# Pools in another order so that matmul operands begin at multiples of 64 bytes, and products over 64 rows filled up to 128 rows with zeros

## The chip, the core and the metric

The kernel runs on one core of a Trainium2 chip. The metric is the device time of one execution in microseconds (us); shorter is better. TensorE (PE) multiplies, ScalarE (ACT), VectorE (DVE) and GpSimd (POOL) do the element-wise work, and SyncE (SP) issues the loads. A product on PE has a stationary operand, which a weight load (PEld) brings into the array, and a moving operand, whose columns stream through it. Both come from the on-chip memory SBUF.

## The reference: what is computed

Two layers of an encoder over 256 tokens of width 2048, all in float32. Each layer is one wide projection, three mixers side by side, an output projection, and a feed-forward block:

```python
def hybrid_layer(x, ...):
    h = rms_norm(x, norm_mix)
    z = jnp.einsum('bsd,de->bse', h, w_in)
    ...
    y_a = mlstm_mixer(ml_q, ml_k, ml_v, ml_o, ml_g, ...)        # 4 heads, d_k 64, d_v 128
    y_b = mla_mixer(mla_cq, mla_ckv, ...)                       # 6 heads, 128 + 64 (rope) per head
    y_c = dilated_mixer(dil_q, dil_k, dil_v, ...)               # 6 heads of 128
    y = jnp.concatenate([y_a, y_b, y_c], axis=-1)
    x = x + jnp.einsum('bse,ed->bsd', y, w_out)
    h = rms_norm(x, norm_ff)
    u = jax.nn.relu(jnp.einsum('bsd,df->bsf', h, w_ff1))        # 2048 -> 8192
    return x + jnp.einsum('bsf,fd->bsd', u * u, w_ff2)
```

## The kernel before

**Precision by splitting.** A float32 operand is kept as two float32r parts, `hi` (ACT rounds) and `lo` (DVE subtracts); a product of two such operands is three matmuls, hi·hi, hi·lo and lo·hi. Each element has 4 bytes in either part.

**Weights.** `Weights` streams all weights in one fixed order in tiles of 128 x 1024. SP loads a tile into one of three `wst` buffers, ACT writes `whi`, DVE writes `wlo` (four buffers each), three tiles ahead of PE.

**Products with weights.** `token_group` serves the input projection (moving `whi` or `wlo`, stationary `xg`), the output projection (stationary `y`) and the second feed-forward product (stationary `u`): for each of 16 row blocks and each of two token halves, two matmuls with `whi` and one with `wlo`, 512 columns each (336 in one of the nine input groups). `w_half` serves the first feed-forward product: weights are stationary, and each row block of `xg` moves once with 512 columns (both parts, against `whi`) and once with 256 (the hi part, against `wlo`). All of these write a tile named `g`.

**Mixers.** Their products stand between those of the next input group. They are generators; a planner (`Stream`) with fixed costs for each engine decides, when the program is written, behind which product each step is put. Room in a pool is counted by `take` and `give`: `t2` has 22 tiles of 2,048 bytes, `half` 7 of 1,024. Two of the mixers' products contract over 64 rows only: in `mla_head` the lo part of the rotated keys (`kr[1]`, tile `krl`, 64 x 256) against `qrT_sb`, twice per head, 12 heads in both layers; in `ml_head` the lo part of q (`ml_ql`, 64 x 256) against `ml_k`, twice per head, 8 heads in both layers. Their neighbours contract over 128 rows (hi and lo one above the other).

**Where tiles lie.** Pools lie in SBUF one behind another in the order in which they are opened, and so do the tiles of a pool. Before, `cp` is first, and in it `vec`, whose row has 952 elements: 3,808 bytes, 59.5 times 64. Nearly every tile behind it therefore begins 32 bytes past a multiple of 64: `xg`, `x`, `whi`, `wlo`, `u`, `y`, all operands of the mixers, and the constants. So do all slices of them that a matmul takes. In the pool `big` a buffer has 4,128 bytes (64.5 times 64, set by `ml_va`), so that every other one begins at a multiple of 64; they hold only float32 sources of transposes and `ml_va`. Counted in 2,048 bytes, `xg`, `whi` and `wlo` begin at the same place (736), the tiles of `t2` (`u`, `y`) at another (1,888).

Of the kernel before, what the change touches and what calls it, by code (L numbers as in the profile page):

```python
# [10 lines left out]
F32 = mybir.dt.float32  # L11
F32R = mybir.dt.float32r
AF = mybir.ActivationFunctionType
# [43 lines left out]
V_BIAS = V_DROPE + 4 * DIL_ROT  # L57
V_ON = V_BIAS + 16
V_ALL = V_ON + ML_H * ML_DV


class Ctx:
# [385 lines left out]

def load_vectors(c, l):

    c.vec = c.cp.tile([P, V_ALL], F32, tag="vec", name="vec", bufs=1)
    c.nc.scalar.dma_start(c.vec[:, :V_GF], c.vecs[l, :, :V_GF])

    def rest():
        c.nc.scalar.dma_start(c.vec[:, V_GF:], c.vecs[l, :, V_GF:])

    return rest

# [74 lines left out]
def k_rope(c, z1):  # L533
    nc = c.nc
    yield from c.s.take(half=1)
    ss = c.small.tile([P, 2], F32, tag="kr_ss", name="kr_ss")
    for tt in range(NT):
        nc.scalar.activation(junk(c, MLA_ROPE), z1[:, tt, :MLA_ROPE], AF.Square, accum_out=ss[:, tt:tt + 1])
    yield
    mean_eps(c, ss, ss, MLA_ROPE)  # L540
    y = yield from rsqrt(c, ss, 2)
    kr = c.half.tile([P, NT, MLA_ROPE], F32, tag="half", name="kr")
    nc.vector.tensor_tensor(out=kr, in0=z1[:, :, :MLA_ROPE],
                            in1=y[:, :2].unsqueeze(2).to_broadcast([P, NT, MLA_ROPE]), op=ALU.mult)
    yield
    apply_rope(c, kr, kr, c.rope[:, 2], c.rope[:, 3], NT, MLA_ROPE)
    yield
    tp = yield from bank(c, "krT")
    for tt in range(NT):
        transpose(c, tp[:MLA_ROPE, tt * P:(tt + 1) * P], kr[:, tt])  # L550

    kh = c.cp.tile([P, S], F32R, tag="krh", name="krh", bufs=1)
    kl = c.cp.tile([MLA_ROPE, S], F32R, tag="krl", name="krl", bufs=1)
    yield
    k = tp[:MLA_ROPE, :S]
    nc.scalar.copy(kh[MLA_ROPE:], k)
    split2(c, kh[:MLA_ROPE], kl, k)
    c.s.give(m=1, half=1)
    c.kr = kh, kl

# [53 lines left out]
def mla_head(c, h):  # L614
    nc = c.nc
    WQ = MLA_NOPE + MLA_ROPE
    NK = MLA_QR // P
    yield from c.s.take(**MLA_ROOM)
    hi, lo = c.w.next()
    if h == MLA_H - 1:  # L620
        c.s.give(t2=4)
    ps = []
    for tt in range(NT):
        b = new_bank(c, "mla_z")
        for kt in range(NK + 1):
            if kt < NK:
                o, cs, first, last = b[:, :WQ], slice(kt * WQ, (kt + 1) * WQ), kt == 0, kt == NK - 1
            else:
                o, cs, first, last = b[:, WQ:WQ + 256], slice(NK * WQ, NK * WQ + 256), True, True
            xh = c.lat[kt][:, tt * P:(tt + 1) * P]  # L630
            xl = c.lat[kt][:, S + tt * P:S + (tt + 1) * P]
            mm(c, o, xh, hi[:, cs], first, False)
            mm(c, o, xh, lo[:, cs], False, False)
            mm(c, o, xl, hi[:, cs], False, last)
        ps.append(b)
    yield

    cols = ((0, MLA_NOPE), (WQ, WQ + MLA_NOPE), (MLA_NOPE, WQ))
    ss = c.small.tile([P, 3, 2], F32, tag="mla_ss", name="mla_ss", bufs=4)
    for tt in range(NT):  # L640
        for i, (a, b) in enumerate(cols):
            nc.scalar.activation(junk(c, b - a), ps[tt][:, a:b], AF.Square, accum_out=ss[:, i, tt:tt + 1])
    vh = c.half.tile([P, NT, MLA_V], F32R, tag="half", name="mla_vh")
    vl = c.half.tile([P, NT, MLA_V], F32R, tag="half", name="mla_vl")
    for tt in range(NT):
        src = ps[tt][:, WQ + MLA_NOPE:WQ + 256]
        nc.vector.tensor_copy(vh[:, tt], src)
        nc.vector.tensor_tensor(out=vl[:, tt], in0=src, in1=vh[:, tt].bitcast(F32), op=ALU.subtract)
    yield
    mean_eps(c, ss[:, 0:2], ss[:, 0:2], MLA_NOPE)  # L650
    mean_eps(c, ss[:, 2], ss[:, 2], MLA_ROPE)
    r = yield from rsqrt(c, ss.rearrange("p a b -> p (a b)"), 6)
    qr = c.tmp.tile([P, NT, MLA_ROPE], F32, tag="qr", name="qr", bufs=3)
    a, b = cols[2]
    for tt in range(NT):
        nc.vector.tensor_scalar(out=qr[:, tt], in0=ps[tt][:, a:b], scalar1=r[:, 4 + tt:5 + tt], scalar2=None,
                                op0=ALU.mult)
    yield
    nk = tile2k(c, "nk", F32).rearrange("p (i t d) -> p i t d", i=2, t=NT)
    for i in range(2):  # L660
        a, b = cols[i]
        for tt in range(NT):
            nc.scalar.activation(nk[:, i, tt], ps[tt][:, a:b], AF.Copy, scale=r[:, 2 * i + tt:2 * i + tt + 1])
    c.s.give(m=2)
    apply_rope(c, qr, qr, c.rope[:, 0], c.rope[:, 1], NT, MLA_ROPE)
    yield
    tp = yield from bank(c, "nkT")
    for i in range(2):
        for tt in range(NT):
            transpose(c, tp[:, i * S + tt * P:i * S + (tt + 1) * P], nk[:, i, tt])  # L670
    yield
    q, k = tile2k(c, "mla_q"), tile2k(c, "mla_k")
    split_gains(c, (q, k), tp, V_NOPE)
    c.s.give(m=1)
    yield
    tq = yield from bank(c, "qrT")
    for tt in range(NT):
        transpose(c, tq[:MLA_ROPE, tt * P:(tt + 1) * P], qr[:, tt])
    yield
    qs = c.half.tile([P, S], F32R, tag="half", name="qrT_sb")  # L680
    split2(c, qs[:MLA_ROPE], qs[MLA_ROPE:], tq[:MLA_ROPE, :S])
    c.s.give(m=1)
    yield
    sc = (yield from bank(c, "mla_s")).rearrange("p (t s) -> p t s", t=NT)
    for tt in range(NT):
        t = slice(tt * P, (tt + 1) * P)
        mm3(c, sc[:, tt], (q[:, t], q[:, S:][:, t]), (k[:, :S], k[:, S:]), True, False)
        mm(c, sc[:, tt], qs[:, t], c.kr[0], False, False)
        mm(c, sc[:, tt], qs[:MLA_ROPE, t], c.kr[1], False, True)
    p = yield from softmax(c, sc, (MLA_NOPE + MLA_ROPE) ** -0.5, None)  # L690
    yield from pv(c, p, [(vh[:, st], vl[:, st]) for st in range(NT)], 4 + h, 3)
    c.s.give(half=3)
# [146 lines left out]
def ml_qk(c, ps, rt):  # L839
# [3 lines left out]
    for tt in range(NT):  # L843
        nc.scalar.activation(z[:, tt], ps[tt], AF.Copy, scale=rt[:, tt:tt + 1])
    yield
    yield from c.s.take(t2=4)
    for pr in range(2):
        tp = yield from bank(c, "ml_qkT")
        for j in range(2):
            for tt in range(NT):  # L850
                transpose(c, tp[:, j * S + tt * P:j * S + (tt + 1) * P],
                          z[:, tt, j * 256 + pr * P:j * 256 + (pr + 1) * P])
        yield

        kk = tile2k(c, "ml_k").rearrange("p (h t) -> p h t", h=2)
        qq = tile2k(c, "ml_q").rearrange("p (h t) -> p h t", h=2)
        ql = c.half.tile([P, S], F32R, tag="ml_ql", name="ml_ql", bufs=2)
        q, k = tp[:, :S], tp[:, S:]
        half = [slice(i * ML_DK, (i + 1) * ML_DK) for i in range(2)]
        for i, r in enumerate(half):  # L860
            nc.scalar.copy(kk[r, i], k[r])
            nc.scalar.copy(qq[r, i], q[r])
            nc.scalar.copy(qq[half[1 - i], i], q[r])
        yield
        for i, r in enumerate(half):
            o = half[1 - i]
            nc.vector.tensor_tensor(out=kk[o, i], in0=k[r], in1=kk[r, i].bitcast(F32), op=ALU.subtract)
            nc.vector.tensor_tensor(out=ql[r], in0=q[r], in1=qq[r, i].bitcast(F32), op=ALU.subtract)
            c.mlqk.append((kk[:, i], qq[:, i], kk[r, i], ql[r]))
        c.s.give(m=1)  # L870


def ml_v(c, ps, rt):
    nc = c.nc
    c.va = c.big.tile([P, NT, ML_H, ML_DV + 1], F32, tag="big", name="ml_va")
    nc.gpsimd.memset(c.va[:, :, :, ML_DV:], 1.0)
    yield
    for tt in range(NT):
# [24 lines left out]

def ml_head(c, h):
    nc = c.nc
    kk, qq, kh, ql = c.mlqk[h]
    yield from c.s.take(t2=2, half=1)
    ws = []
    for d in range(2):
# [13 lines left out]
    st = yield from bank(c, "ml_st")  # L923
    for s in range(NT):
        mm(c, st[:, s * S:(s + 1) * S], kk[:, s * P:(s + 1) * P], qq, True, False)
        mm(c, st[:, s * S:(s + 1) * S], kh[:, s * P:(s + 1) * P], ql, False, True)
    yield
    stv = st.rearrange("p (s t) -> p s t", s=NT)
    sc = ML_DK ** -0.5
# [11 lines left out]
    c.s.give(m=1)  # L941
    c.mlqk[h] = None
    if c.mlqk[h ^ 1] is None:
        c.s.give(t2=2)
    hs = c.half.tile([P, NT, ML_DV], F32, tag="half", name="ml_hs")
    ss = c.small.tile([P, 2], F32, tag="ml_ss", name="ml_ss", bufs=4)
    C1 = ML_DV + 1
# [184 lines left out]
def encoder(ctx, tc, xT, x, const, vecs, w_in, w_in1, w_mla, w_out, w_ff1, w_ff2, out):  # L1132
# [7 lines left out]
        vecs, w_in, w_in1, w_mla, w_out, w_ff1, w_ff2, out)  # L1140
    c.B_ST, c.B_HL = 3, 4
    pool = lambda name, bufs, **k: ctx.enter_context(tc.tile_pool(name=name, bufs=bufs, **k))
    c.cp = pool("cp", 1)
    c.small = pool("small", 2)
    c.tmp = pool("tmp", 2)
    c.xp = pool("xp", 1)
    c.wp = pool("wp", 1)
    c.big = pool("big", 4)
    c.half = pool("half", HALF)
    c.t2 = pool("t2", T2)  # L1150
    c.gps = pool("gps", 4, space=PSUM)
    c.mps = pool("mps", 4, space=PSUM)
    ctx.enter_context(tc.manual_schedule())
# [171 lines left out]
```

## Time and profile before

| | |
|---|---|
| median of 3 runs | 2199.95 us (2199.28 to 2200.12) |
| the profiled execution: its own time | 2200.16 us |
| its span (first to last instruction) | 2197.9 us |
| PE busy | 2164.0 us, 98% of the span |
| DVE busy / ACT busy / POOL busy | 1326.9 / 1077.9 / 110.9 us |
| DMA engines | 56.2% busy with the weights' queue, 177 GB/s on average |

The first 33 us are the start, the mixers of the two layers lie at about 33 to 300 us and 1145 to 1390 us, each followed by the output projection (70 us) and four rounds of the two feed-forward products. A PE duration in the profile overlaps the next instruction's, and its end is modelled; the pace of PE is read from the starts.

### The profile page before, as it was taken

The page shows a single profiled execution, that of the slowest core. Times are in us where ns is not written, and L with a number is a line of the kernel's source. Part 1 is how long each engine was busy: PE and PEld are TensorE (multiplying, and loading weights), DVE is VectorE, ACT ScalarE, POOL GpSimd, SP SyncE. Part 2 cuts the span into 40 slices and gives each one's busy share as a digit, 9 for nine tenths or more (in the row PEclk, how much of TensorE's full clock was granted, in tenths as well). Part 3 has the DMA queues.
Part 4 walks back from the last instruction along what each step waited for, and adds up shares of the span by engine and source line. Part 5 has one row for each costly group of instructions (what it writes and reads, how often), then busy time and mean ns, then how long its engine had stood idle before and what let it go on. Part 6 is the DMA issues. An engine that isn't in the chain of part 4 may idle for free.

```text
span 2197.9 us, 28890 instructions
## 1 busy us (share of the span) xinstructions
PE 2164.0 (98%) x10848; PEld 1805.4 (82%) x10848; DVE 1326.9 (60%) x1963; ACT 1077.9 (49%) x1873; POOL 110.9 (5%) x142
## 2 busy tenths in 40 slices
PE   8999999999999999999999999999999999999999
PEld 6787888888888888888887888888888888888887
DVE  7667755655564565565557687556546645655654
ACT  5666655543443444344456666454434434534442
POOL 6112100000000000000001021000000000000000
PEclk9999999999999999999999999999999999999999
DMA  7543455565666656566554434556566666666564
GB/s 233 183 139 109 157 175 175 184 190 186 188 185 189 190 184 190 183 191 192 173 172 156 126 122 154 172 182 191 183 192 184 190 182 192 184 189 190 185 198 156
DMA packets 109004, 389.89 MB, mean 177 GB/s; under 512 B 12352, under 2 KB 12480, under 8 KB 108608
## 3 DMA queue, kind: packets, MB, share of 16 engines
q1 hardware_dynamic: 107136, 384.97, 56.2%
q10 hardware_dynamic: 1728, 3.07, 0.4%
q8 instruction: 85, 1.39, 0.3%
q14 instruction: 55, 0.45, 0.1%
HBM read 385.90 MB, written 2.10 MB: 177 GB/s over the span
## 4 chain that ended last, share of the span: by engine, by line
PE 91%; ACT 3%; DVE 2%; POOL 2%; issue 1%; DMA 1%; POOLq 0%; ACTq 0%; SPq 0%; DVEq 0%
PE g L193 85%; PE mla_z L193 1%; ACT whi L97 1%; PE mla_s L193 1%; ACT junk L97 1%; POOL acc L97 1%; DMA wst<-w_in 1%; PE oT L193 1%; POOL sq L97 1%; DVE wlo L97 1%; PE ml_h L193 1%; PE xT L199 0%; PE ml_st L193 0%; PE pT L199 0%; PE dil_s L193 0%
## 5 line engine op out<-in xcount | busy, mean ns | idle before, releaser
L97 DVE TENSOR_TENSOR wlo<-wst,whi 128x1024 fp32r<-128x1024 f32 (+2 forms) x732 | 889.7, 1223 | 436.8 <-ACT whi L97 427.6
L97 ACT CAST whi<-wst 128x1024 fp32r<-128x1024 f32 (+2 forms) x732 | 759.8, 1041 | 667.5 <-PE g L193 553.4
L193 PE MATMUL g<-xg,whi 128*128 128x512 f32 x2048 | 714.7, 398 | 2.9 <-DVE xg L97 2.9
L193 PE MATMUL g<-whi,u 128*128 128x512 f32 x2048 | 646.0, 395 | 0.0
L193 PE MATMUL g<-xg,wlo 128*128 128x256 f32 x2048 | 554.3, 281 | 0.0
L193 PEld LDWEIGHTS g<-whi,u 128*128 128x128 f32 x2048 | 384.5, 188 | 92.7
L193 PEld LDWEIGHTS g<-xg,whi 128*128 128x128 f32 x2048 | 376.6, 188 | 86.3 <-DVE xg L97 3.4
L193 PE MATMUL g<-wlo,u 128*128 128x512 f32 x1024 | 404.5, 395 | 0.0
L193 PEld LDWEIGHTS g<-xg,wlo 128*128 128x128 f32 x2048 | 386.6, 189 | 12.6
L193 PE MATMUL g<-whi,xg 128*128 128x512 f32 (+1 forms) x1152 | 373.2, 390 | 6.7 <-ACT whi L97 6.7
L193 PEld LDWEIGHTS g<-whi,xg 128*128 128x128 f32 x1152 | 215.4, 189 | 46.1 <-ACT whi L97 6.7
L193 PEld LDWEIGHTS g<-wlo,u 128*128 128x128 f32 x1024 | 192.3, 188 | 46.2
L193 PE MATMUL g<-wlo,xg 128*128 128x512 f32 (+1 forms) x576 | 221.7, 385 | 3.8 <-DVE wlo L97 3.8
L97 ACT COPY ev<-g 128x256 f32<-128x256 f32 x128 | 47.7, 372 | 241.4 <-PE g L193 241.4
L193 PE MATMUL g<-whi,y 128*128 128x512 f32 x512 | 165.2, 397 | 0.0
L97 DVE TENSOR_TENSOR ev<-g,ev 128x256 f32<-128x256 f32 x128 | 54.3, 424 | 132.3 <-ACT ev L97 132.3
L193 PEld LDWEIGHTS g<-wlo,xg 128*128 128x128 f32 x576 | 109.0, 189 | 23.4 <-DVE wlo L97 6.9
L193 PEld LDWEIGHTS g<-whi,y 128*128 128x128 f32 x512 | 96.5, 188 | 21.8
L193 PE MATMUL g<-wlo,y 128*128 128x512 f32 x256 | 101.0, 395 | 0.0
L97 DVE SCALAR_TENSOR_TENSOR x<-g,r,x 128x512 f32<-128x512 f32 x64 | 46.5, 751 | 87.9 <-PE g L193 87.9
L97 DVE SCALAR_TENSOR_TENSOR ev<-ev 128x256 f32<-128x256 f32 x128 | 54.5, 426 | 4.4
L193 PEld LDWEIGHTS g<-wlo,y 128*128 128x128 f32 x256 | 48.3, 189 | 10.4
(204 smaller groups left out, 1196.3 us busy)
## 6 DMA issues: line engine op xcount, KB each, us to landing
wst<-w_ff SPq DMA_DIRECT2D x512, 512.0 KB, 3.9
wst<-w_in SPq DMA_DIRECT2D x128, 512.0 KB, 3.6
wst<-w_out SPq DMA_DIRECT2D x64, 512.0 KB, 4.1
wst<-w_in SPq DMA_DIRECT2D x16, 336.0 KB, 3.0
wst<-w_mla SPq DMA_DIRECT2D x12, 416.0 KB, 3.2
xt<-xT SPq DMA_DIRECT2D x8, 256.0 KB, 5.4
x<-x SPq DMA_DIRECT2D x2, 1024.0 KB, 7.9
out<-x ACTq DMA_DIRECT2D x8, 256.0 KB, 2.1
```

The costliest lines, as they stand in the source:

```text
L97: return fn(*args, **kw)
L193: c.nc.tensor.matmul(out, lhsT, rhs, start=start, stop=stop)
```

## The change

The pools are opened in another order, `xp`, `wp`, `t2`, `half` and `tmp` ahead of `cp`, and the row of `vec` is rounded up to 960 elements, that of `ml_va` to 1040. In the program as built every operand of a matmul then begins at a multiple of 64 bytes but for slices of `ml_va`, of a 4-column operand and of the one-column selectors; `xg`, `whi`, `wlo` and the tiles of `t2` begin at the same place counted in 2,048 bytes (128). The lo part of the rotated keys gets 128 rows, of which ACT fills 64 with zeros once per layer, and the matmul takes all 128 rows of `qrT_sb`. `ml_ql` becomes a tile of `t2` with 128 rows per head, of which ACT fills 64 with zeros (four times per layer), and its matmul takes all 128 rows of `ml_k`. `ml_qk` asks for six tiles of `t2` at once instead of four.

```diff
+V_PAD = -(-V_ALL // 16) * 16
...
-    c.vec = c.cp.tile([P, V_ALL], F32, tag="vec", name="vec", bufs=1)
+    c.vec = c.cp.tile([P, V_PAD], F32, tag="vec", name="vec", bufs=1)
...
-    kl = c.cp.tile([MLA_ROPE, S], F32R, tag="krl", name="krl", bufs=1)
+    kl = c.cp.tile([P, S], F32R, tag="krl", name="krl", bufs=1)
+    nc.scalar.activation(kl[MLA_ROPE:], c.const[MLA_ROPE:, :S], AF.Copy, scale=0.0)
...
-    split2(c, kh[:MLA_ROPE], kl, k)
+    split2(c, kh[:MLA_ROPE], kl[:MLA_ROPE], k)
...
-        mm(c, sc[:, tt], qs[:MLA_ROPE, t], c.kr[1], False, True)
+        mm(c, sc[:, tt], qs[:, t], c.kr[1], False, True)
...
-    yield from c.s.take(t2=4)
+    yield from c.s.take(t2=6)
...
-        ql = c.half.tile([P, S], F32R, tag="ml_ql", name="ml_ql", bufs=2)
+        ql = tile2k(c, "ml_ql").rearrange("p (h t) -> p h t", h=2)
...
+            nc.scalar.activation(ql[half[1 - i], i], q[r], AF.Copy, scale=0.0)
...
-            nc.vector.tensor_tensor(out=ql[r], in0=q[r], in1=qq[r, i].bitcast(F32), op=ALU.subtract)
-            c.mlqk.append((kk[:, i], qq[:, i], kk[r, i], ql[r]))
+            nc.vector.tensor_tensor(out=ql[r, i], in0=q[r], in1=qq[r, i].bitcast(F32), op=ALU.subtract)
+            c.mlqk.append((kk[:, i], qq[:, i], ql[:, i]))
...
-    c.va = c.big.tile([P, NT, ML_H, ML_DV + 1], F32, tag="big", name="ml_va")
+    va = c.big.tile([P, 1040], F32, tag="big", name="ml_va")[:, :NT * ML_H * (ML_DV + 1)]
+    c.va = va.rearrange("p (t h d) -> p t h d", t=NT, h=ML_H)
...
-        mm(c, st[:, s * S:(s + 1) * S], kh[:, s * P:(s + 1) * P], ql, False, True)
+        mm(c, st[:, s * S:(s + 1) * S], kk[:, s * P:(s + 1) * P], ql, False, True)
...
-        c.s.give(t2=2)
+        c.s.give(t2=3)
...
+    c.xp = pool("xp", 1)
+    c.wp = pool("wp", 1)
+    c.t2 = pool("t2", T2)
+    c.half = pool("half", HALF)
+    c.tmp = pool("tmp", 2)
     c.cp = pool("cp", 1)
     c.small = pool("small", 2)
-    c.tmp = pool("tmp", 2)
-    c.xp = pool("xp", 1)
-    c.wp = pool("wp", 1)
     c.big = pool("big", 4)
-    c.half = pool("half", HALF)
-    c.t2 = pool("t2", T2)
```

The order of PE's instructions differs at one place in each layer, where the transposes `ml_qkT` of the second half of q and k are put. On PE in the first layer, before the change, from the products ahead of `ml_qkT` to the first product of an `mla_head`:

```order
L193 MATMUL g<-whi,xg 128x512
L199 MATMUL ml_qkT<-const,ml_z 128x128 x4
L193 MATMUL g<-whi,xg 128x512
L193 MATMUL g<-wlo,xg 128x512
L193 MATMUL g<-whi,xg 128x512 x2
L193 MATMUL g<-wlo,xg 128x512
L193 MATMUL g<-whi,xg 128x512
L193 MATMUL mla_s<-mla_k,mla_q 128x256 x3
```

The same place with the change:

```order
L194 MATMUL g<-whi,xg 128x512 x2
L194 MATMUL g<-wlo,xg 128x512
L194 MATMUL g<-whi,xg 128x512 x2
L194 MATMUL g<-wlo,xg 128x512
L194 MATMUL g<-whi,xg 128x512
L200 MATMUL ml_qkT<-const,ml_z 128x128 x4
L194 MATMUL g<-whi,xg 128x512
L194 MATMUL g<-wlo,xg 128x512
L194 MATMUL g<-whi,xg 128x512 x2
L194 MATMUL g<-wlo,xg 128x512
L194 MATMUL g<-whi,xg 128x512
L194 MATMUL mla_s<-mla_k,mla_q 128x256 x3
```

Six products with weights more stand ahead of `ml_qkT` and of the `mla_s` behind it; six fewer stand between `mla_s` and the transposes of its softmax. On ACT at that place, before the change, the first half of q and k and the cast of the next weight tile:

```order
L97 CAST whi<-wst 128x1024
L97 CAST ml_k<-ml_qkT 64x256
L97 CAST ml_q<-ml_qkT 64x256 x2
L97 CAST ml_k<-ml_qkT 64x256
L97 CAST ml_q<-ml_qkT 64x256 x2
L97 CAST whi<-wst 128x832
L97 CAST qrT_sb<-qrT 64x256
```

With the change:

```order
L98 CAST whi<-wst 128x1024
L98 CAST ml_k<-ml_qkT 64x256
L98 CAST ml_q<-ml_qkT 64x256 x2
L98 ACTIVATE ml_ql<-ml_qkT 64x256
L98 CAST ml_k<-ml_qkT 64x256
L98 CAST ml_q<-ml_qkT 64x256 x2
L98 ACTIVATE ml_ql<-ml_qkT 64x256
L98 CAST whi<-wst 128x832
L98 CAST qrT_sb<-qrT 64x256
```

Two fills with zeros (`ml_ql`) are new in the row; what follows them moves back by two instructions.

## Rows read from the trace of the kernel before

**Rows 1.** The page: PE's busy time, and the chain that ended last, by line

```profile
PE 2164.0 (98%) x10848; PEld 1805.4 (82%) x10848; DVE 1326.9 (60%) x1963; ACT 1077.9 (49%) x1873; POOL 110.9 (5%) x142
PE g L193 85%; PE mla_z L193 1%; ACT whi L97 1%; PE mla_s L193 1%; ACT junk L97 1%; POOL acc L97 1%; DMA wst<-w_in 1%; PE oT L193 1%; POOL sq L97 1%; DVE wlo L97 1%; PE ml_h L193 1%; PE xT L199 0%; PE ml_st L193 0%; PE pT L199 0%; PE dil_s L193 0%
```

**Rows 2.** Groups on PE by form: count | busy us, mean ns | idle before

```profile
L193 PE MATMUL g<-xg,whi 128*128 128x512 f32 x2048 | 714.7, 398 | 2.9 <-DVE xg L97 2.9
L193 PE MATMUL g<-whi,u 128*128 128x512 f32 x2048 | 646.0, 395 | 0.0
...
L193 PE MATMUL g<-whi,xg 128*128 128x512 f32 x1024 | 343.3, 399 | 6.7 <-ACT whi L97 6.7
...
L193 PE MATMUL g<-whi,y 128*128 128x512 f32 x512 | 165.2, 397 | 0.0
...
L193 PE MATMUL mla_s<-krl,qrT_sb 64*128 64x256 f32 x24 | 9.1, 381 | 0.0
...
L193 PE MATMUL ml_st<-ml_ql,ml_k 64*128 64x256 f32 x16 | 6.1, 380 | 0.0
```

**Rows 3.** Timeline of PE in the second feed-forward product (start us, us)

```profile
499.70 0.63 PE L193 MATMUL g<-whi,u 128*128 128x512 f32 x2
...
500.40 0.63 PE L193 MATMUL g<-whi,u 128*128 128x512 f32 x2
```

**Rows 4.** The same in the first feed-forward product

```profile
600.61 0.40 PE L193 MATMUL g<-xg,whi 128*128 128x512 f32 x1
...
601.67 0.40 PE L193 MATMUL g<-xg,whi 128*128 128x512 f32 x1
```

**Rows 5.** The same in an input group of the second layer

```profile
1205.57 0.62 PE L193 MATMUL g<-whi,xg 128*128 128x512 f32 x2
...
1206.93 0.62 PE L193 MATMUL g<-whi,xg 128*128 128x512 f32 x2
```

**Rows 6.** Busy time by stretch, with granted clock, DMA share and GB/s

```profile
104.80:106.50 1.70, 1.70 (x9) 1.70 (x9) 0.94 (x2) 1.70 (x3) 0.00 (x0) 0.50 0.06 14
...
400.00:460.00 60.00, 60.00 (x341) 52.03 (x341) 38.66 (x54) 29.51 (x43) 0.00 (x0) 1.00 0.61 190
```

**Rows 7.** Timeline of PE, products of an mla_head, in the first stretch of rows 6

```profile
105.20 0.41 PE L193 MATMUL mla_z<-wlo,lat_hl 128*128 128x192 f32 x1
...
105.84 0.41 PE L193 MATMUL mla_z<-wlo,lat_hl 128*128 128x192 f32 x1
```

**Rows 8.** Timeline of PE, the same products of another head

```profile
67.50 0.27 PE L193 MATMUL mla_z<-wlo,lat_hl 128*128 128x192 f32 x1
...
68.17 0.28 PE L193 MATMUL mla_z<-wlo,lat_hl 128*128 128x192 f32 x1
```

**Rows 9.** Timeline of PE around a product over 64 rows in mla_head

```profile
96.43 0.28 PE L193 MATMUL mla_s<-krh,qrT_sb 128*128 128x256 f32 x1
96.63 0.38 PE L193 MATMUL mla_s<-krl,qrT_sb 64*128 64x256 f32 x1
96.94 0.50 PE L193 MATMUL g<-whi,xg 128*128 128x512 f32 x1
97.28 0.40 PE L193 MATMUL g<-wlo,xg 128*128 128x512 f32 x1
```

**Rows 10.** Timeline of PE, the four products ml_st of a head and what follows

```profile
170.28 0.39 PE L193 MATMUL ml_st<-ml_q,ml_k 128*128 128x256 f32 x1
...
171.53 0.50 PE L193 MATMUL g<-whi,xg 128*128 128x512 f32 x1
171.87 0.39 PE L193 MATMUL g<-wlo,xg 128*128 128x512 f32 x1
```

**Rows 11.** Whom PE waited for: total us, times, longest us

```profile
PE pT L199 <- DVE sm_e L97: 2.1, 2, 1.1
...
PE ml_qkT L199 <- DVE qrT_sb L97: 1.5, 2, 0.8
```

**Rows 12.** A copy of 64x256 on ACT: ns min/median/max, first and last start

```profile
L97 ACT CAST ml_q<-ml_qkT x16: 364/367/369, 89.7 to 1187.2; 64x256 fp32r<-64x256 f32 x16
```

More of the change, by code (lines that the diff above doesn't have):

```diff
@@ L449, in load_vectors @@
 def load_vectors(c, l):
-    c.vec = c.cp.tile([P, V_ALL], F32, tag="vec", name="vec", bufs=1)
+    c.vec = c.cp.tile([P, V_PAD], F32, tag="vec", name="vec", bufs=1)
     c.nc.scalar.dma_start(c.vec[:, :V_GF], c.vecs[l, :, :V_GF])
     def rest():
-        c.nc.scalar.dma_start(c.vec[:, V_GF:], c.vecs[l, :, V_GF:])
+        c.nc.scalar.dma_start(c.vec[:, V_GF:V_ALL], c.vecs[l, :, V_GF:])
     return rest
@@ L905, in ml_head @@
     nc = c.nc
-    kk, qq, kh, ql = c.mlqk[h]
+    kk, qq, ql = c.mlqk[h]
     yield from c.s.take(t2=2, half=1)
```

## The prediction

> **What bounds the kernel now.** I read the page first. PE is busy for 98% of the span, and products with weights make 85% of the chain that ended last [rows 1]; what happens to PE's pace is what happens to the time. The durations say nothing of that pace, since each overlaps the next instruction's (395 to 399 ns for 512 columns [rows 2]). So I went to the timeline and took starts.
>
> In the second feed-forward product three matmuls of 512 columns follow each other in 0.70 us, 233.3 ns each [rows 3]. In the first one, three pairs of 512 and 256 columns take 1.06 us, 353.3 ns a pair [rows 4]; less 233.3 that leaves 120 for 256 columns. In an input group six matmuls of 512 take 1.36 us, 226.7 ns each [rows 5]. At the upper level of 2.4 GHz, which is granted there (1.00 in [rows 6]), 512 columns at one a cycle are 213.3 ns and a pair is 320. So every product with weights pays 13 to 33 ns that its columns don't explain: the 2,048 products from `u` (with as many again by half for `wlo`, 3,072) 20 each, the 2,048 pairs 33 each, and so on, some 170 us in all.
>
> Is this excess the array's or that of the operands' supply? Between 104.8 and 106.5 us the clock was at its lower level (0.50 [rows 6]); there three matmuls of 192 columns take 0.64 us, 213 ns each, which is 256 cycles of 1.2 GHz [rows 7]. The same products at the upper level take 0.67 us for six, 111.7 each [rows 8], where half of 213 would be 106.7. The array's part halves with the clock; 5 ns don't. I read these 192-column products as paced by their weight loads, since their columns alone would need only 160 ns at 1.2 GHz. So there is a part that shows only when PE asks for its operands at full speed, and supply is where I look. In an input group the excess is 13.3 ns on 213.3, one in sixteen: one cycle more for every 16 columns, and 16 columns are 64 bytes. All operands there begin 32 bytes off a multiple of 64. That fits a cost for reading across a 64-byte border. It doesn't prove one: a cost that every 64 bytes have wherever they begin would look the same, and no float32r product of this trace has an aligned operand to compare.
>
> **Part 1: the alignment.** The trace lacks the operation, so I bound it from both sides. The lower end is no excess at all: 213.3 for 512 columns, 106.7 for 256. The upper end is no change. I take 215 and 111 ns: for 512 columns near the floor, because the excess has just the size that the border explains, and for 256 columns the 111.7 of a product that waits for its weight load [rows 8], which may or may not shrink with it. By stage, with counts from [rows 2] (`wlo` has half the count of `whi`, as the code issues two to one, and in the first feed-forward product as many):
> - second feed-forward product, 3,072 x (233.3 - 215) = 56.2 us;
> - first one, 2,048 pairs x (353.3 - 326) = 55.9 us;
> - output projection, 768 x 18.3 = 14.1 us, at the pace of [rows 3], since its stationary operand lies in the same pool;
> - input groups, 1,536 x (226.7 - 215) = 18.0 us;
> - the 336-column group and the mixers' products of 256, some 500 x 8 ns = 4 us.
>
> That is 148 us. About 5 go into waits that don't shorten: the first 33 us, where PE starts at the loads' pace, and chains through ACT and DVE in the mixers. 143 are left. Nothing else becomes the bound: in the heaviest feed-forward stretch DVE is busy 38.66 of 60 us and the DMA share is 0.61 [rows 6], and at 92% of the time these become 0.70 and 0.66.
>
> The Trainium skill ("TensorE: Matmul & The Clock Gate", section Back-to-back issue gap) gives N/2.4 + 2.5 ns for the gap between products at the upper level, 215.8 for 512 columns. This trace is 11 to 18 above it. With 215.8 and 109.2 the sum would be 142 instead of 148, an estimate from that page.
>
> **Part 2: 64 rows made 128.** Here the trace has both kinds side by side. In `mla_head` the full product ahead of the one with 64 rows takes 0.20 us until the next start, the 64-row one 0.31, and the full one behind it 0.34 [rows 9], where 0.12, 0.12 and 0.23 are usual (above): 0.38 too much. The array seems to empty between the two shapes. With 24 of these [rows 2] that is 9.1 us. In `ml_head` four products take 1.25 us and the next 0.34 [rows 10], instead of 0.48 and 0.23: 0.88 a head, 8 heads, 7.0 us. Columns and weight loads stay the same in number, so full shape gives back 16 us. The bounds are 14 (some heads begin without the longer first product) and 17.
>
> **Part 3: fills, room, order.** Ten fills of 64 x 256 on ACT at 0.37 us [rows 12] are 3.7 us, on an engine that is busy for half of the span. They matter at one place in each layer: behind two of them stand a weight cast and the cast of `qrT_sb`, whose lo part on DVE `ml_qkT` waits for on PE (1.5 us in both layers [rows 11]). That chain becomes 0.73 us longer, but the planner now puts six products more (1.36 us) ahead of `ml_qkT`, so that wait shrinks. The same six are missing between `mla_s` and the transposes `pT`, which wait 2.1 us in both layers now [rows 11]; that wait can grow by 1.36 per layer. From -3.6 (both gone) to +2.7; I take 0. The room of six in `t2` changes no other place of PE's order. SP's order is the same.
>
> **Sum.** 2200.2 (the profiled execution's own time, 0.2 above the median of the runs) - 143 - 16 + 0 = 2041 us.
>
> **The rivals.**
> - *The excess goes in part.* If it is the weight load's reading beside the stream that costs, a shorter read saves some of it, not all. [Rows 3] against [rows 5] speak for more than one cause: the same products with the same moving tiles differ by 6.7 ns, only the pool of the stationary operand being another. Half of 148 is 74: 2200 - 74 - 16 = 2110 us, with 2080 to 2150 for a third to three quarters left.
> - *The reorder doesn't do what it says.* If the excess belongs to float32r at full pace wherever operands begin, only part 2 remains: 2200 - 16 = 2184 us, within 3. For it speaks that nothing in this trace shows an aligned product running faster. The Trainium skill ("SBUF — State Buffer", Specifications) has lines of 16 bytes, and all operands begin at multiples of 16 already; by that rule this case comes out. Against it: the excess is one cycle to 64 bytes, and no 16-byte border explains that.
> - *Slower.* Now `xg`, `whi`, `wlo`, `u` and `y` all begin at the same place in 2,048 bytes. If a weight load and a stream that run through the same places hinder each other, each of the 7,424 products of 512 columns could pay the 6.7 ns by which places already tell [rows 3, 5]: +50 - 16, 2234 us. It decides from 2.2 ns per product on. Against it: in the input groups the two operands begin at the same place already, and those are the fast ones [rows 5].
>
> **How the numbers follow.** The excess goes almost wholly (2015 to 2075): 48%. In part: 21%. Nothing but part 2: 25%. Slower: 4%. The rest, 2%, is a new wait in the mixers that eats part 2. The likeliest gives 2041 us, by itself 2015 to 2075. The range has to reach the case of part 2 alone, which holds more than I may leave out: 2015 to 2188. A measurement of this kernel can tell about 0.2% (4 us) from no change. The first three cases are all faster by more, 93% with a little lost to waits; 3% within 0.2%; 4% slower.
>
> **What would show it.** Part 1 is right if starts in the second feed-forward product lie 214 to 217 ns apart and pairs in the first 320 to 330, with the input groups no longer faster than the output projection. If they stay at 233 and 353, the alignment does nothing; at 224 and 338 half of it. Part 2 is right if the products `mla_s` and `ml_st` start 0.11 to 0.12 us apart throughout. Part 3 is right if `pT` and `ml_qkT` wait no more than 6 us together. I would be wrong if DVE or the loads appear as what PE waits for in the feed-forward products, or if products become unequal by place in a new way.

## The result and the profile after

The changed kernel takes 2169.26 us (median of 4 runs, 2168.57 to 2171.6) beside 2200.03 us for the kernel before in the same series: 0.9861 of it, 95% interval 0.9844 to 0.9878, or 31 us less. The profiled execution took 2168.57 us. The forecast was 2041 us: the direction is right and the time lies in the range, but the gain is a fifth of the one forecast.

The page of the changed kernel, PE's busy line and the chain by line (compare [rows 1]):

```profile
PE 2130.9 (98%) x10848; PEld 1803.9 (83%) x10848; DVE 1326.0 (61%) x1963; ACT 1082.7 (50%) x1883; POOL 110.0 (5%) x142
PE g L194 84%; PE mla_z L194 1%; ACT junk L98 1%; ACT whi L98 1%; DVE wlo L98 1%; PE oT L194 1%; POOL acc L98 1%; POOL sq L98 1%; DMA wst<-w_in 1%; PE xT L200 0%; PE dil_s L194 0%; PE pT L200 0%; PE mla_s L194 0%; POOL rp L98 0%; ACT dil_z L98 0%
```

The bound has not moved: PE is still busy for 98%, and weights' products make up 84% of the chain. So the pace has to be read again from starts. The timeline of PE in the changed kernel (start us, us, line, operation, tiles, form, count), one piece each from the mixers, the second feed-forward product, the first one and an input group:

```profile
168.06 0.28 PE L194 MATMUL mla_s<-krh,qrT_sb 128*128 128x256 f32 x1
168.17 0.28 PE L194 MATMUL mla_s<-krl,qrT_sb 128*128 128x256 f32 x1
168.30 0.52 PE L194 MATMUL mla_s<-mla_k,mla_q 128*128 128x256 f32 x3
...
168.89 0.28 PE L194 MATMUL ml_st<-ml_q,ml_k 128*128 128x256 f32 x1
169.01 0.28 PE L194 MATMUL ml_st<-ml_ql,ml_k 128*128 128x256 f32 x1
...
490.28 0.62 PE L194 MATMUL g<-whi,u 128*128 128x512 f32 x2
...
490.96 0.62 PE L194 MATMUL g<-whi,u 128*128 128x512 f32 x2
...
589.72 0.40 PE L194 MATMUL g<-xg,whi 128*128 128x512 f32 x1
...
590.78 0.40 PE L194 MATMUL g<-xg,whi 128*128 128x512 f32 x1
...
1193.26 0.62 PE L194 MATMUL g<-whi,xg 128*128 128x512 f32 x2
...
1194.62 0.62 PE L194 MATMUL g<-whi,xg 128*128 128x512 f32 x2
```

Three products of the second feed-forward product take 0.68 us, 226.7 ns each, where [rows 3] had 0.70. Three pairs of the first one still take 1.06 us [rows 4], and six products of an input group still 1.36 us [rows 5], though their operands moved from 32 bytes past a multiple of 64 to multiples of 64. The products that now have 128 rows follow each other at 0.11 to 0.13 us, where [rows 9, 10] had 0.20 to 0.31.

Added up by stage, from the first start of one stage to the first of the next (the last one to its last start):

| stages, us | before | after | difference | forecast |
|---|---|---|---|---|
| input groups and mixers (2) | 548.6 | 540.1 | -8.5 | about -33 |
| output projections (2) | 191.3 | 187.6 | -3.7 | -14.1 |
| first feed-forward products (8) | 728.0 | 728.7 | +0.7 | -55.9 |
| second feed-forward products (8) | 718.9 | 699.1 | -19.8 | -56.2 |

What PE waited for in the changed kernel (total us, times, longest us), and the stretches behind the waits (us, busy time of PE, PEld, DVE, ACT, POOL, granted clock, DMA share, GB/s):

```profile
PE pT L200 <- DVE sm_e L98: 5.8, 2, 2.9
...
PE stat L194 <- POOL acc L98: 1.7, 1, 1.7
```

```profile
36.80:40.20 3.40, 3.40 (x14) 3.40 (x14) 2.83 (x8) 1.43 (x4) 3.40 (x9) 0.50 0.18 32
...
105.10:108.50 3.40, 3.40 (x16) 3.40 (x17) 1.40 (x3) 1.96 (x3) 0.00 (x0) 0.50 0.02 7
...
1176.80:1183.60 6.80, 6.37 (x27) 5.51 (x27) 3.88 (x7) 3.28 (x6) 0.00 (x0) 0.50 0.00 0
```

`pT` waits 2.9 us in each layer, where it waited 2.1 in both together [rows 11]; that of `ml_qkT` is gone from the list. Behind each of these waits PE runs at the lower clock (0.50), 13.6 us in all; in the kernel before it was one stretch of 3.4 us, that of [rows 6].

### The profile page after: what moved, and what is told of

Read it like the earlier page. It is cut to its first block, busy times and chain, and to the rows that moved or that the text cites. A ratio compares the mean times of both kernels' runs of the same rounds, so it can differ in the third digit from the quotient of the medians.

```text
span 2166.3 us, 28896 instructions
## 1 busy us (share of the span) xinstructions
PE 2130.9 (98%) x10848; PEld 1803.9 (83%) x10848; DVE 1326.0 (61%) x1963; ACT 1082.7 (50%) x1883; POOL 110.0 (5%) x142
## 4 chain that ended last, share of the span: by engine, by line
PE 89%; ACT 4%; DVE 3%; POOL 2%; issue 1%; DMA 1%; POOLq 0%; SPq 0%; ACTq 0%; DVEq 0%
PE g L194 84%; PE mla_z L194 1%; ACT junk L98 1%; ACT whi L98 1%; DVE wlo L98 1%; PE oT L194 1%; POOL acc L98 1%; POOL sq L98 1%; DMA wst<-w_in 1%; PE xT L200 0%; PE dil_s L194 0%; PE pT L200 0%; PE mla_s L194 0%; POOL rp L98 0%; ACT dil_z L98 0%
## 5 line engine op out<-in xcount | busy, mean ns | idle before, releaser
L194 PE MATMUL g<-whi,u 128*128 128x512 f32 x2048 | 633.8, 389 | 0.0
L194 PE MATMUL g<-wlo,u 128*128 128x512 f32 x1024 | 398.4, 389 | 0.0
```

The costliest lines, as they stand in the source:

```text
L194: c.nc.tensor.matmul(out, lhsT, rhs, start=start, stop=stop)
```

## The experiments

Sixteen runs; the kernel before ran beside each, and ratios are to it. The *distance* of two operands is the number of bytes by which their starts in a partition differ; section 1 below finds distances of 0 and 256 alike, so it is counted up to 256. Operands at distance 0 begin at the same *place*.

### 1. The pace of one product by itself

A kernel of nothing but products, 48 to a stage, with the two operands placed at chosen distances (its loop, shortened):

```python
for i in range(48):
    a, b = (i % 2) * 512 + m // 4, (i % 3) * 256 + s // 4      # m, s: offsets in bytes
    nc.tensor.matmul(g[:w, :c], st[:, b:b + w], mv[:, a:a + c], start=i == 0, stop=i == 47)
```

> Not the reference's work: 26 rows of 48 products each, on one tile of moving and one of stationary operands, with the starts of both moved by bytes, and with other numbers of columns; the output is the input. Theory border (an operand that begins off a multiple of 64 bytes costs): both_at_half slower than both_at_zero, by up to 13 ns of 227. Theory place (what counts is how far apart the two operands begin, in some power of two of bytes): both_at_half the same as both_at_zero, 226.7 ns each, and sta_plus_two (128 bytes apart, as u and whi were before) 233 ns, half_sta_plus_two too. Theory contention (the other engines' traffic costs): 213 to 216 ns in all rows without traffic, 227 to 236 in the busy ones. If the excess is one cycle in sixteen of the stream, 256, 336 and 384 columns take 113, 149 and 170 ns; if it is 32 cycles per product, 120, 153 and 173. If it is the weight load's, it falls by half with 64 columns of weights and to a quarter with 32.

The timeline of PE, one merged row to a stage; the distance between the starts of two rows over 48 is the pace:

```profile
21.87 11.05 PE L88 MATMUL both_at_zero<-mv,st 128*128 128x512 f32 x48
32.76 11.07 PE L88 MATMUL both_at_half<-mv,st 128*128 128x512 f32 x48
43.66 11.36 PE L88 MATMUL mov_zero_sta_half<-mv,st 128*128 128x512 f32 x48
...
66.07 11.36 PE L88 MATMUL sta_plus_line<-mv,st 128*128 128x512 f32 x48
77.26 11.32 PE L88 MATMUL sta_plus_two<-mv,st 128*128 128x512 f32 x48
...
99.42 11.07 PE L88 MATMUL sta_plus_four<-mv,st 128*128 128x512 f32 x48
110.33 11.32 PE L88 MATMUL sta_plus_six<-mv,st 128*128 128x512 f32 x48
...
143.87 8.48 PE L88 MATMUL cols_a<-mv,st 128*128 128x384 f32 x48
152.19 7.52 PE L88 MATMUL cols_b<-mv,st 128*128 128x336 f32 x48
159.55 5.92 PE L88 MATMUL cols_c<-mv,st 128*128 128x256 f32 x48
165.30 5.91 PE L88 MATMUL cols_c_half<-mv,st 128*128 128x256 f32 x48
```

Both operands at multiples of 64 or both 32 bytes past one: 226.9 and 227.1 ns, the same. The stationary operand 64 bytes on, with both aligned: 233.1; 256 bytes on: 227.3. So a border of 64 bytes costs nothing, and the distance of the two operands costs 6 to 7 ns. Only below 32 bytes did the start itself count: both operands 16 bytes past a multiple of 32 took 233.3. Theory contention failed: beside copies, subtractions and a load the stages took 227.2 to 227.3 at distance 0, as without them. And the 13.3 ns that are left are no cycle in sixteen: 384, 336 and 256 columns take 173.3, 153.3 and 119.8 ns, each 13.1 to 13.3 above its columns at 2.4 GHz, that is 32 cycles whatever the number of columns. Weights of 64 or 32 columns instead of 128 took 230 and 232 ns, no less. Products of 512 bf16 columns started 216 ns apart. The Trainium skill ("TensorE: Matmul & The Clock Gate", section Back-to-back issue gap) gives 215.8 ns for 512 columns as the gap of an isolated product; the bf16 stage agrees, the float32r products of this case do not: 226.7 is the fastest that a run of them alone reached.

### 2. The parts apart, and the place without the alignment

The rows alone (`krl` and `ml_ql` with 128 rows, pools as before):

> The change without the reorder of the pools: only the products of 64 rows are made 128. My prediction's part 2 says 16 us less than before, 2184 us. If what the input stage shows after the whole change (8.5 us less in both layers together) is all of it, because waits of the softmax transposes and stretches at the lower clock give the rest back, 2191 us. Pace in the second feed-forward product as before, 233 ns.

2191.92 us (2190.0 to 2195.39), ratio 0.9957 (0.9942 to 0.9972). The pools alone:

> The reordered pools alone; products of 64 rows stay at 64 rows (the tile of ml_va is padded 32 bytes less, so that all fits). If the two parts add up, this gives what is left of the gain of 30.8 us after the 8.3 of the rows alone: 2177 us, 2174 to 2180, with 226.7 ns in the second feed-forward product and one stretch at half clock as in the kernel before. Rival (the parts need each other, since pools fix where ml_ql lies): under 18 us or over 27 us gained.

2178.58 us (2176.53 to 2182.34), ratio 0.9907 (0.989 to 0.9923). The two ratios multiply to 0.9864, and the change has 0.9861: the parts add. With the pools alone the input groups and mixers take 548.2 us, 0.4 less than before: alignment gave nothing there.

All operands moved 32 bytes off again, at the same places relative to each other:

```diff
+    pool("shift", 1).tile([P, 8], F32, name="shift")
     c.xp = pool("xp", 1)
```

> The changed kernel with 32 unused bytes ahead of all pools, so that every operand again begins 32 bytes off a multiple of 64, at the same distances from each other. Theory border: the second feed-forward product and the output projection go back from 226.7 to 233.3 ns a product, 2169 + 25 = 2195 us. Theory place: nothing moves, 226.7 ns and 2169 us.

2170.44 us (2170.03 to 2172.6), ratio 0.986 (0.9845 to 0.9874): the whole gain stays without the alignment to 64 bytes. And everything aligned, but `t2` (`u`, `y`), and with it the pools behind it, 128 bytes further on, the distance that the kernel before had, counted in 512 bytes:

```diff
     c.wp = pool("wp", 1)
+    pool("shift", 1).tile([P, 32], F32, name="shift")
     c.t2 = pool("t2", T2)
```

> The changed kernel with 128 unused bytes between the weights' pool and t2, so that all operands keep multiples of 64 bytes, but u and y begin 128 bytes away from whi and wlo (counted in 512 bytes), as before the change. Theory border: nothing moves, 226.7 ns and 2169 us. Theory place: 233.3 ns in the second feed-forward product and the output projection, 2195 us.

2192.0 us (2191.25 to 2192.47), ratio 0.9955 (0.9938 to 0.9971): the gain of the pools is gone (the input groups, whose operands did not move against each other, kept 226.7). PE's timeline in the second feed-forward product, first of the kernel shifted by 32:

```profile
489.95 0.61 PE L194 MATMUL g<-whi,u 128*128 128x512 f32 x2
...
490.63 0.61 PE L194 MATMUL g<-whi,u 128*128 128x512 f32 x2
```

then of the aligned kernel with `t2` at 128:

```profile
489.64 0.63 PE L194 MATMUL g<-whi,u 128*128 128x512 f32 x2
...
490.34 0.63 PE L194 MATMUL g<-whi,u 128*128 128x512 f32 x2
```

0.68 us for three without that alignment, 0.70 with it. What the pools' new order did was to bring `u` and `y` to the weights' place. The Trainium skill ("SBUF — State Buffer", Specifications) has lines of 16 bytes, by which all operands were aligned before; that starts 32 bytes past a multiple of 64 did as well as multiples of 64 (2170.44 and 2169.26 us) agrees with it.

### 3. Distances, pairs and phase

The first feed-forward product had distance 0 in both kernels and paid 353.3 ns a pair. A second kernel of products alone took more distances, and alternating 512 and 256 columns:

> A kernel of nothing but stages of 48 float32r products (128 weight columns; it computes none of the reference). Single stages have 512 columns each, at a distance of the stationary from the moving operand's start that is 0 to 448 bytes; the at_ stages move both starts; pair stages alternate 512 and 256 columns as the first feed-forward product does, some with one product of 192 or 128 columns ahead to start them in another phase, some beside copies on ACT, subtractions on DVE and a load. Place theory: 226.7 ns at distances 0 and 256 and 229 to 233.3 at all others, whatever the absolute place, except where starts are not at multiples of 32 bytes. Rival (absolute places): at_one_one and at_two_two differ from single_zero. For pairs, phase theory: 346.7 or 353.3 ns a pair at one and the same distance, by how the stage starts and by what runs beside it; rival (distance): some distances give 346.7 in every start and beside the other engines, others 353.3 in every start.

For 512 columns the place theory held (226.7 at 0 and 256, also with both starts moved by 64 or 128; 228.8 at 192 and 448; 232.4 to 234.4 at the others). Equal places are not enough where the starts are off a multiple of 32: both at 16 took 231.1 here, both at 48 230.0. Pairs are another matter. PE's timeline of some stages of 24 pairs:

```profile
221.23 8.49 PE L67 MATMUL pair_zero_a<-mv,st 128*128 128x512 f32 x48
229.56 0.25 PE L59 MATMUL ahead<-mv,st 128*128 128x192 f32 x1
...
238.00 0.22 PE L59 MATMUL ahead<-mv,st 128*128 128x128 f32 x1
238.06 8.69 PE L67 MATMUL pair_zero_c<-mv,st 128*128 128x512 f32 x48
246.59 8.64 PE L67 MATMUL pair_one_a<-mv,st 128*128 128x512 f32 x48
...
467.43 8.32 PE L67 MATMUL pair_one_zero<-mv,st 128*128 128x512 f32 x48
475.59 8.64 PE L67 MATMUL busy_zero<-mv,st 128*128 128x512 f32 x48
484.07 8.63 PE L67 MATMUL busy_one<-mv,st 128*128 128x512 f32 x48
```

At distance 0 the same pairs run at 347 ns (8.33 us for 24) or, after one product of 128 columns, at a steady 353.3 (8.53 with its start). Nothing ran beside them; beside copies, subtractions and a load they took 353.3. So at distance 0 the pace depends on how a run starts, which the texts here call its *phase* (no view shows it directly), and it then stays. At 64 and 192 bytes the rival held: 353.2 to 353.8 in all three starts, and at 128 350.8 in all three. One mixed setting, `whi` 64 bytes from `xg` and `wlo` at 0, gave 340.0 (8.16 us for 24). A third kernel looked at all such settings:

> Stages of 48 float32r products again (it computes none of the reference). Pair stages alternate 512 and 256 columns as the first feed-forward product does, with whi and wlo each at its own distance from xg, 0 to 224 bytes in steps of 32; the ahead_ stages repeat some of them after a product of 128 columns, so that they start in another phase; the three stages go as the second feed-forward product does (x high with whi, x high with wlo, x low with whi), at each distance of x from whi and of wlo from whi, some with the low half of x moved too. Place theory in its fuller form: a pair with whi 64 bytes past xg and wlo at 0 takes 340 ns in either start (it was 342.8 with its first products, against 353.3 in the kernel), and the threes have a setting of their own below 226.7 ns. Rival (a fixed cost): no stage of threes goes below 226.7 ns, which is 512 columns and 32 cycles, and the pair of 340 was one start's luck: in the other start it takes 347 to 356.

The rival came true in both points. The best pair is again `whi` at 64, `wlo` at 0: 340.0, but 350.0 in the other start; `whi` at 192, `wlo` at 0 had 350.0 and 340.0, the other way round; `whi` at 0 and `wlo` at 64 took 346.7 in both. No stage of threes was below 226.7. Distance 0 took 353 without a product ahead and 346 with one, the reverse of the second kernel: the product ahead does not fix the pace by itself, and no view shows what else does. Two of these settings in the real kernel, moved in the first feed-forward product alone (shown for `wlo`; for `whi` it is the mirror image):

```diff
-        lo = c.wp.tile([P, 1024], F32R, tag="wlo", name="wlo", bufs=c.B_HL)
+        oh, ol = self.srcs[self.k][2:] or (0, 0)
+        lo = c.wp.tile([P, 1088], F32R, tag="wlo", name="wlo", bufs=c.B_HL)[:, ol:]
...
-            srcs += [(c.w_ff1[l, ch * KT + i, half], 1024) for i in range(KT) for half in range(2)]
+            srcs += [(c.w_ff1[l, ch * KT + i, half], 1024, 0, 16) for i in range(KT) for half in range(2)]
```

> The changed kernel with wlo 64 bytes further on in the first feed-forward product alone (whi and xg as they are; all other products keep distance 0). Place theory: pairs go from 353.3 to 346.7 ns, as in the stages with 0 and 64 in both starts, and 2,048 of them give 13.7 us: 2155.5 us, 2153 to 2159. Rival (the kernel's pairs are slow for what else runs then, loads and casts): pairs stay at 353, 2168 to 2171.

2167.98 us (2166.83 to 2169.4), ratio 0.985 (0.9836 to 0.9863): a miss. The stages' 346.7 came only in the first group of 16 pairs of six of the eight stages, all other groups took 353.3. The time fits the rival, but its cause, loads and casts, is not shown by it: they ran beside the first groups too.

> The same with whi 64 bytes further on and wlo as it is. Place theory: pairs of 340 or 350 ns, as in the two starts of the stages with 64 and 0; up to 27 us less if the kernel's start falls as the stage's first did, 2142 us, and 7 us less, 2162, if as its second. Rival (loads and casts): 353, 2168 to 2171.

2158.33 us (2155.5 to 2160.25), ratio 0.9805 (0.9791 to 0.9818), pairs 347.8 in the mean. PE's timeline there, four pairs from row to row, in three groups that follow each other:

```profile
556.76 0.39 PE L194 MATMUL g<-xg,whi 128*128 128x512 f32 x1
...
558.12 0.39 PE L194 MATMUL g<-xg,whi 128*128 128x512 f32 x1
...
562.58 0.40 PE L194 MATMUL g<-xg,whi 128*128 128x512 f32 x1
...
563.99 0.40 PE L194 MATMUL g<-xg,whi 128*128 128x512 f32 x1
...
568.57 0.40 PE L194 MATMUL g<-xg,whi 128*128 128x512 f32 x1
...
569.97 0.40 PE L194 MATMUL g<-xg,whi 128*128 128x512 f32 x1
```

1.36, 1.41 and 1.40 us: 340, 353 and 350 ns a pair, and so on in a cycle of three. Each group keeps one pace, and the next begins with another. Every group ends with its last two products in the other order (`wlo` first). The same with one even order instead:

```diff
-        if end:
-            mm(c, ps[:, :S], wl, acts[k0 + k][:, :S], False, False)
-        mm(c, ps, wh, acts[k0 + k], first and k == 0, end)
+        mm(c, ps, wh, acts[k0 + k], first and k == 0, False)
+        mm(c, ps[:, :S], wl, acts[k0 + k][:, :S], False, end)
         if not end:
-            mm(c, ps[:, :S], wl, acts[k0 + k][:, :S], False, False)
             c.s.pump()
```

> The changed kernel with whi 64 bytes further on in the first feed-forward product, and every group of it in one even order of 512 and 256 columns (the last product of a group is now the one with wlo, no longer the one with whi). Phase theory: a pace that has set in is kept through all groups of a stage, so that each of the eight stages has one pace, 340, 350 or 353 ns, and not a cycle of three: 2131 us less than all at 340 can't be, 2143 us with all at 340, 2168 with all at 353; about 2150. Rival (ends of groups cost by themselves, and the cycle goes on): three paces in turn as now, 2156 to 2160.

2150.29 us (2147.04 to 2152.56), ratio 0.9766 (0.9753 to 0.9779). Six of the eight stages run at 340 throughout (86.94 us from their first to their last start), the first of each layer at 353 and 350. The same at distance 0:

> The changed kernel with the even order alone, whi and wlo at 0. Phase theory: each stage at 346.7 or 353.3 throughout, 2155 to 2169 us. Rival: 353.3 in all groups as now, 2168 to 2171.

2168.59 us (2166.55 to 2171.18), ratio 0.9853 (0.9839 to 0.9866): the first stage of each layer at 347 throughout, the other six at 353. Phase theory holds in both: an even order keeps the phase in which a stage starts, good or bad. The even order with `wlo` at 64 was not run.

### 4. Where half of the 128 rows' gain went

The products `mla_s` and `ml_st`, each run of them with the product behind it, took 37.2 us of PE from start to start before and 21.7 after: 15.5 of the forecast 16 us are saved, but the two input stages show only 8.5. First the fills, as they are but outside the planner's count (the same instruction through the plain engine object), which puts `ml_qkT` back six products:

> The changed kernel with the ten zero fills on ACT as they are, but issued past the planner, which then puts ml_qkT where the kernel before had it (six products earlier) and mla_s six products ahead of pT again. Wait theory: pT waits for sm_e 5.8 -> about 2 us in all, ml_qkT waits again, 1.5 to 3 us, and at most one stretch at half clock is left: 2160 us, 2157 to 2164. Rival (the wait moves): ml_qkT's wait takes back what pT's loses and as many stretches at half clock stay: 2168 to 2172.

2171.39 us (2169.18 to 2173.18), ratio 0.9868 (0.9853 to 0.9882): the rival. `pT` waits 3.5 us and `ml_qkT` 2.6. Then on POOL:

> The same order of products, with the ten fills on POOL, so that ACT's chain to ml_qkT is as short as in the kernel before. Wait theory: pT waits about 2 us, ml_qkT 1.5, 2158 us, 2155 to 2163, 1 to 3 below the one with uncounted fills. Rival (the fills collide with POOL's rotation of qr and with dil_z, or with DVE's work): no better than uncounted fills, with dqkT's wait for dil_z above 4.5 us.

2168.66 us (2166.46 to 2169.1), ratio 0.9854 (0.9839 to 0.9868): a miss, and no difference from the change that these runs can tell, though `pT` waits 3.5 us instead of 5.8; nor did the rival's collision come, as `dqkT` waits 4.4. PE's order is that of before here. In the first layer the `mla_s` ahead of `pT`, with the product behind them, take 1.42 us instead of 2.18, and `pT` waits 1.78 us instead of 1.08: of 0.76 us saved 0.70 come back as a wait. The timeline of DVE ahead of `pT` in this kernel (start us, us; idle time ahead would stand in brackets):

```profile
99.77 1.21 DVE L98 TENSOR_TENSOR wlo<-wst,whi 128x1024 fp32r<-128x1024 f32 x1
101.01 0.42 DVE L98 TENSOR_TENSOR ml_k<-ml_qkT,ml_k 64x256 fp32r<-64x256 f32 x1
...
102.31 0.43 DVE L98 TENSOR_TENSOR ml_ql<-ml_qkT,ml_q 64x256 fp32r<-64x256 f32 x1
102.77 0.17 DVE L98 RECIPROCAL sm<-sm 128x2 f32<-128x2 f32 x1
102.97 0.62 DVE L98 TENSOR_SCALAR sm_e<-sm_e,sm 128x256 f32<-128x256 f32 x2
```

DVE stands without a gap: it is what sets the pace here, and a PE that reaches `pT` earlier only waits longer. So the next kernel was to put the subtractions for `ml_k` and `ml_ql` behind the softmax, by a later due time:

```diff
+        c.s.cur.last["act"] = c.s.cur.last.get("act", c.s.clk) + 3.5
         yield
```

> The kernel with the fills on POOL, and the casts and subtractions of ml_k, ml_q and ml_ql put behind the softmax of the same stretch on ACT and DVE (a due time 3.5 us later for ml_qk's last step; ml_qkT moves behind mla_s on PE). Queue theory: pT waits under 1 us in all instead of 3.5, the stretches at half clock of 3.4 and 6.8 us near 105 and 1177 us go, and the time falls by 2.5 + 5 us: 2161 us, 2158 to 2164. Rival (the wait moves on): ml_qkT or oT waits instead, as many stretches at half clock, 2166 to 2170.

2165.47 us (2164.71 to 2166.91), ratio 0.9839 (0.9825 to 0.9852): 3 us below the fills on POOL, though the intervals overlap. The trace shows that half of what was meant came about. The subtractions of the second half of q and k went behind the softmax; those of the first half took their place on DVE, ahead of the softmax's reciprocal, and what moved out of this stretch is the subtraction `wlo` of a weight tile:

```profile
97.04 0.42 DVE L98 TENSOR_TENSOR ml_k<-ml_qkT,ml_k 64x256 fp32r<-64x256 f32 x1
...
98.80 0.17 DVE L98 RECIPROCAL sm<-sm 128x2 f32<-128x2 f32 x1
```

From the last `mla_s` on PE to the start of `pT` 4.1 us pass instead of 5.1. `pT` waits 2.0 us in all, but a new wait stands beside it:

```profile
PE oT L194 <- DVE mla_k L98: 3.0, 2, 1.5
...
PE pT L200 <- DVE sm_e L98: 2.0, 2, 1.0
```

The lower clock stayed in stretches of 3.4, 3.4 and 6.8 us. Both theories were partly right: the shorter queue shortened `pT`'s wait by 1.5 us in all, and 3.0 us came elsewhere. On ACT the casts of the second half (98.02 to 100.05 us) now stand ahead of those of `mla_q` and `mla_k`, and DVE waits 1.3 us for these. An order with all eight subtractions behind the softmax was not run. With `wlo` at 64 as well:

> wlo at 64 bytes in the first feed-forward product and the softmax first, fills on POOL. If the two add: 2148 us, 2143 to 2154. Rival (either fails): what the other run alone gives.

2164.11 us (2161.97 to 2164.92), ratio 0.9829 (0.9816 to 0.9843), as `wlo` gave nothing. Last, everything that helped, with `whi` at 64 and the even order:

> whi at 64 bytes, the even order, the fills on POOL and the softmax first. If the gains add: 3 to 4 us below the first of these runs. Rival: no lower than that one.

2143.2 us (2141.25 to 2145.85), ratio 0.9737 (0.9724 to 0.9751), 7 us below the same without the softmax first, where 3 to 4 were forecast (by the stages 6.0 in the input stages, 0.9 in the first feed-forward products), and 26 below the change: faster than both kernels. Its pairs, six from the first row to the last:

```profile
589.70 0.39 PE L194 MATMUL g<-xg,whi 128*128 128x512 f32 x1
...
591.74 0.39 PE L194 MATMUL g<-xg,whi 128*128 128x512 f32 x1
```

2.04 us, 340 ns a pair, where [rows 4] had 353.3; its first feed-forward products take 706.9 us instead of 728.0.

## Why the prediction was wrong, point by point

**What bounds the kernel** was right: PE, through the pace of the weights' products, with 13 to 33 ns each above the columns. That it is an excess that only shows at full pace was right too: in the stretch of the changed kernel at granted clock 0.50 from 36.8 us on, products of 336 columns follow each other at 280 ns, which is 336 cycles of 1.2 GHz and no more. That all of it can be taken away was not right.

**Part 1 failed at "That fits a cost for reading across a 64-byte border".** The size (13.3 on 213.3) was one in sixteen only because the product had 512 columns; 256 columns in a run of their own carry the same 13 ns. The trace before held products of 336 columns, whose pace would have told a constant from a rate. Three of them from row to row there:

```profile
37.95 0.32 PE L193 MATMUL g<-wlo,xg 128*128 128x336 f32 x1
...
38.41 0.32 PE L193 MATMUL g<-wlo,xg 128*128 128x336 f32 x1
```

0.46 us is 153.3 ns each, 13.3 above 140; one cycle in sixteen would be 148.8. The shift by 32 shows that the alignment to 64 bytes did nothing at all. What gained was the place: `u` and `y` came to the weights' place in 256 bytes, 3,072 x 6.6 = 20.3 us and, as the output projection stood at 232.5 before and not at the 233.3 that the prediction took, 768 x 5.8 = 4.5 us; 23.5 by the stages. The prediction had the clue in its hand: "the same products with the same moving tiles differ by 6.7 ns, only the pool of the stationary operand being another" [rows 3, 5]. It was used for the rival of an excess that goes in part and for the one that is slower; the latter had the sign turned round, since the same place is the fast one, as its own last sentence says of the input groups. Read as the cost of a distance, it gives 25 us and, with part 2, 2159 us. Of the 148 us forecast 23 came: output projection and second feed-forward product went to the input groups' pace, and input groups and the first feed-forward product, already at distance 0, stayed. The sign that the input groups would no longer be faster than the output projection came true, for this other reason.

That 2169 us lies in the range is luck as far as part 1 goes: the range reached to 2188 for the case of part 2 alone, and the 23 us beside it came from a cause that the prediction did not forecast. The estimate by the page's gap should be 146 us and not 142, which leaves out the mixers' 4.

**Part 2** was right in mechanism and size: the products follow each other at 0.12 us, and 15.5 us of PE's time went.

**Part 3, taken as 0, was mis-sized:** about 7 us of the 15.5 did not reach the input stages' time. It saw the wait of `pT` grow by up to 1.36 us a layer for the six products that are missing, but not that DVE's queue sets the time of `pT`: what PE saves ahead of it comes back as a wait, 5.8 instead of 2.1 us. Nor did it count the lower clock behind such waits, 10.2 us more at half clock in the two profiled executions, so at most 5.1. Its own sign, that `pT` and `ml_qkT` wait no more than 6 us together, came true (5.8) and did not see this. 15.5 less 3.7, less 0.7 for `stat`, plus the 1.5 of `ml_qkT`, is 12.6; the stages show 8.5, so 4.1 are left for the clock. That share is not measured by itself, but the runs bear on it: of 33 executions of the kernel before in the series of the experiments, the four with a mean granted clock of 1.000 took 2198.5 us in the mean and the five with 0.997 took 2202.7, that is 4.2 us for 0.003 of 2200, 6.6 us of lost clock. Two thirds of 5.1 is 3.3, an estimate. The wait of `stat` (1.7 us) is there with the pools alone too.

**The rivals.** None came out as written. "Nothing but part 2", 2184 us, was nearest in mechanism, for the alignment did nothing; it lacked the place's 23 us and had part 2 whole. The new wait in the mixers, left at 2%, took half of part 2.

**Open.** Why a distance of 64 to 192 bytes costs 2 to 8 ns, why pairs have several steady paces, and what the constant 32 cycles of a float32r product are, no run tells. The first stage of each layer runs in another phase than those behind it; in its trace transposes (`xT`) and a wait of 1.45 us stand among its first products, and in the others not, but that these set the phase was not tested.

## What to carry to other kernels

Before putting an excess down to a rate, read it at two sizes of the same operation: a constant and a share look alike at one size. For products that follow each other back to back, compare where the stationary and the moving operand begin, counted in 256 bytes, and not only how each is aligned; the same products with operands from another pool are the experiment that a trace already holds. And a gain on PE in front of a busy queue of another engine is worth only what that queue lets through: look there first for what it will wait for.

## What was not expected of the hardware

- 512 columns of float32r at equal places: 226.7 ns (544 cycles of 2.4 GHz); with the stationary operand 64 bytes on 233.3, 128 on 232.4, 192 on 228.8, 256 on 226.7. Alignment to 32 bytes was enough; both 16 bytes past a multiple of 32 took 231.1 and 233.3.
- Alternating 512 and 256 columns have more than one steady pace at some settings (346.7 or 353.3 ns a pair at distance 0; 340.0, 350.0 or 353.3 with `whi` 64 bytes off), by how the run starts, and in an even order keep it for all 256 pairs of a stage; 340.0 came only with `whi` 64 or 192 bytes off the place at which single products are fastest.
- A pair of 340.0 (113.3 and 226.7) is below the sum of its products by themselves at their best, 119.8 and 226.7: the 32 cycles belong to a run of equal products, not to every product.
